# RWKV-7 layer: the second four key blocks ordered behind the norm of the first four, and r's weights split three and four pieces ahead

## The chip, the cores and the metric

The kernel runs on one core of one Trainium2 chip. The metric is the device time of one execution in microseconds (us), as the median of several runs. The core's engines each work through a queue of their own, in order: PE (TensorE, matmuls and transposes), DVE (VectorE), ACT (ScalarE), POOL (GpSimd) and SP (SyncE, which issues most of the loads). An instruction waits on semaphores for those on other engines whose results it needs.

## The reference

The model has two mixing layers, each followed by a gated conv-MLP, on 512 tokens of 1024 features: first an RG-LRU layer, then an RWKV-7 layer. The change lies in the RWKV-7 layer, of which this is the part that matters:

```python
rkv = jnp.einsum('sbtd,sde->sbte', xs_rkv, w_rkv)
r, k, v = rkv[0], rkv[1], rkv[2]
w = -jax.nn.softplus(-(w0 + jnp.tanh(xw @ w1) @ w2).astype(f32)) - 0.5
decay = jnp.exp(-jnp.exp(w))
a = jax.nn.sigmoid((a0 + (xa @ a1) @ a2).astype(f32))
kk = (kf * k_k).reshape(bsz, seq, RWKV_H, RWKV_N)
kk = kk / jnp.maximum(jnp.linalg.norm(kk, axis=-1, keepdims=True), 1e-12)
kf = kf * (1.0 + (a - 1.0) * k_a)
y = _rwkv7_scan(rh, hs(decay), kh, vh, -kk, kk * ah)
# one step of the scan, for each of 16 heads of 64:
#   sa = S a_t;  S = S * w_t + sa b_t + v_t k_t;  y = S r_t
```

`kk` is normalised within each head, which needs the sum of squares of 64 features, and then a reciprocal.

## The kernel before

**Stages.** The stages run one after the other: the RG-LRU layer, its conv-MLP, the RWKV-7 layer (here from about 540 to 800 us), the second conv-MLP. A big product is in float32 accuracy from three matmuls: each operand is split in a high part and the rest, and `mm3` (L81) multiplies high by high, high by low and low by high. A weight comes in pieces of 512 KB that are numbered in the order of use. Each is loaded (`raw`, by SP), its high part is cast on ACT (`wh`, L123) and its low part made on DVE (`wl`, L127). `next_weights(ahead=2)` hands out piece i after it has put loads up to piece i + 3 and splits up to piece i + 2 in the queues (with an `ahead` of 4 or more, loads up to i + `ahead` + 2). All raw pieces, splits and many other tiles share one pool of 24 buffers (`b4`), so a load is issued when a buffer of the pool comes free.

**The RWKV-7 layer here.** The projections run in the order k (two products of four blocks of 128 features each), r (two products), v. Pieces 105 to 112 are k's, 113 to 120 are r's, and those from 121 on v's. The mixed inputs of a projection (`mt`, then its split `mix`) are made beside the product before it.

**What prepares the keys.** `prepare(g)` in `rwkv_krv` (L1193) works on four of the eight blocks: g = 0 on the first four, g = 1 on the second. For each block b it makes exp of the running log decay and of its negative (`pinv` L1241 and `ppad` L1244, ACT), the square of the scaled keys (`sq` L1242, ACT), the factor of the second key (`fac` L1243, ACT), then `kp` (L1252, DVE), the other key's product (L1253, DVE), a copy of `ppad` (L1255, on ACT for g = 0, on DVE for g = 1) and two more products (L1257 and L1258, DVE), and PC (L1259, ACT). The squares are summed by a matmul (`ssq`, L1251). Behind the four blocks follows the norm, one dependent chain: ACT copies ssq to `tmp` (L1262), PE transposes it (`sst`, L1266), DVE takes the maximum and two reciprocals (L1268, L1270), PE transposes back (`rec`, L1274), ACT and DVE split it (L1276, L1277), PE spreads it over the heads (`knb`, L1283), and DVE multiplies it in (L1284). Two buffers each of ppad and pinv and one each of fac and kp serve all eight blocks.

**The solve.** `solve(H, ...)` makes the matrices of the heads: matmuls `aab` (L1353), copies of them on ACT (D0, DA and O, L1358 to L1362), a transpose on DVE (`A`, L1366), then a chain of pairs of DVE steps (L1374 and L1376) that invert a triangle row by row in X, then two transposes (LT, L1379, and XN, L1381). PE takes XN with the matmul `m1p` (L1400), and POOL makes the next solve's X out of LT. DVE also does for each chunk the products `W` (L1497) and `tu` (L1579), which PE takes in `tr` (L1504) and `pe` (L1534); `pd` (L1572) and `s` (L1490) lie between.

**Order.** The program is written as tasks that yield; `project` steps the tasks on two lanes while it issues its matmuls. `prepare(0)` and `prepare(1)` stand on lane 0 and `solve(0)` on lane 1:

```python
        self.push(prepare(0))
        ...
        self.push(prepare(1))
        self.push(self.solve(0, AR, BK, LTs), 1)
        self.project(mr, lambda o, ps: ev_r(o, ps), rate=0.4, rate1=1.2)
        self.project(mr, lambda o, ps: ev_r(4 + o, ps), after=trail(2, mv, (4, 2, 2, 2)), rate=1.3, rate1=0.9)
```

The order of the code is not yet that of the queues: a scheduler (Tile) orders each engine's instructions by when its model sees them ready, and the kernel can add a dependency without a semaphore ("NOSYNC") that only fixes an order.

Of the kernel before, what the change touches and what calls it, by code (L numbers as in the profile page):

```python
# [9 lines left out]
AF = mybir.ActivationFunctionType  # L10
ALU = mybir.AluOpType
# [3 lines left out]
NOSYNC = mybir.DependencyInfo(mybir.DependencyClass.NoSync, mybir.DependencyReason.DATA)  # L15
# [7 lines left out]
C = 64  # L23
# [3 lines left out]
DECAY_C = 0.6065306597126334  # L27
# [44 lines left out]
class Kernel:  # L72
# [991 lines left out]
    @staticmethod  # L1064
    def bytok(t):
        return t.rearrange("p (c q t) -> p c q t", q=2, t=C)
# [127 lines left out]
    def rwkv_krv(self, pool, mk, mr, AR, BK, PC, selk, LTs):  # L1194

        nc = self.nc

        def t(tag, bufs):
            return pool.tile([P, T], F32, tag=tag, name=tag, bufs=bufs)


        sel = pool.tile([P, 4, 40], F32, name="sel")
        n8 = pool.tile([P, 4, 40], F32, name="n8")
        for m in (sel, selk, n8):
            nc.gpsimd.memset(m, 0.0)
        for e in range(2):
            hb = slice(e * 64, e * 64 + 64)
            for b in range(4):
                for part in (0, 32):
                    c = part + 2 * b + e  # L1210
                    nc.gpsimd.memset(sel[hb, b, c : c + 1], 1.0)
            for b in range(KB):
                nc.gpsimd.tensor_copy(selk[hb, b, e : e + 1], self.vec("rwkv_r_k", b)[hb])
        backs = []

        def selection():
            psb = self.bank("back")
            for j in range(4):
                nc.tensor.transpose(psb[0:40, j * P : (j + 1) * P], sel[:, j, :], self.ident)
            backs.append(self.b4(F32R, (4 * P,), "back")[0:40])  # L1220
            nc.scalar.copy(backs[0], psb[0:40, :])

        ppads = [pool.tile([P, NC, C + 1], F32, name=f"ppad{i}") for i in range(2)]
        for pp in ppads:
            nc.vector.memset(pp[:, :, 0:1], 1.0)
        bytok = self.bytok

        def prepare(g):


            ssq = self.bank("ssq")
            sqs = []
            for j in range(4):
                b = g * 4 + j
                pad = ppads[b % 2]
                pp = pad.rearrange("p (c q) t -> p c q t", q=2)
                Lc, rr, a, ko = self.inner(AR, b), self.outer(AR, b), self.inner(BK, b), self.outer(BK, b)
                if j % 2 == 0:
                    two = self.b4(F32, (2, T), "sq")
                sq, pinv, fac, kp = two[:, j % 2], t("pinv", 2), t("fac", 1), t("kp", 1)  # L1240
                nc.scalar.activation(bytok(pinv), Lc, AF.Exp, scale=DECAY_C)  # L1241
                nc.scalar.activation(bytok(sq), ko, AF.Square, scale=self.vec("rwkv_k_k", b))  # L1242
                nc.scalar.activation(bytok(fac), a, AF.Identity, bias=self.oka[:, b : b + 1], scale=self.vec("rwkv_k_a", b))  # L1243
                nc.scalar.activation(pp[:, :, :, 1:], Lc, AF.Exp, scale=-DECAY_C)  # L1244
                yield 1
                if g == 0 and j == 2:
                    selection()

                sqs.append(sq)
                for i in (3, 0, 1, 2) if j == 3 else ():  # L1250
                    (self.tc.keep_in_program_order if i < 3 else lambda ins: ins)(nc.tensor.matmul(ssq[32 * i : 32 * i + 32, :], sel[:, 0, 0:32], sqs[i], start=True, stop=True, tile_position=(0, 32 * i)))  # L1251
                nc.vector.tensor_tensor(bytok(kp), ko, bytok(pinv), ALU.mult)  # L1252
                nc.vector.scalar_tensor_tensor(a, a, self.vec("rwkv_k_k", b), bytok(kp), ALU.mult, ALU.mult)  # L1253
                yield 1
                (nc.vector.tensor_copy if g else nc.scalar.copy)(rr, pp[:, :, :, 1:])  # L1255
                self.done.add(("r", b))
                nc.vector.tensor_tensor(Lc, ko, pp[:, :, :, 0:C], ALU.mult)  # L1257
                nc.vector.tensor_tensor(ko, bytok(kp), bytok(fac), ALU.mult)  # L1258
                nc.scalar.copy(PC[:, b, :], pad[:, :, C])  # L1259
                yield 1  # L1260
            ss = t("tmp", 1)
            nc.scalar.copy(ss, ssq)  # L1262
            yield 1
            pt = self.bank("sst")
            for c in range(4):
                nc.tensor.transpose(pt[:, c * P : (c + 1) * P], ss[:, c * P : (c + 1) * P], self.ident)  # L1266
            pv = pt.rearrange("p (c j w) -> p c j w", c=4, w=32)[:, :, :, 0:2]
            nc.vector.tensor_scalar(n8[:, :, 0:8].rearrange("p c (j e) -> p c j e", e=2), pv, 1e-24, None, ALU.max)  # L1268
            for part in (32, 0):
                nc.vector.reciprocal(n8[:, :, part : part + 8], n8[:, :, 0:8])  # L1270
            yield 1
            pr = self.bank("rec")
            for c in range(4):
                nc.tensor.transpose(pr[0:40, c * P : (c + 1) * P], n8[:, c, :], self.ident)  # L1274
            rec = self.b4(F32R, (T,), "rec")[0:40]
            nc.scalar.copy(rec, pr[0:40])  # L1276
            nc.vector.tensor_tensor(rec[32:40], pr[32:40], rec[32:40].bitcast(F32), ALU.subtract)  # L1277
            yield 1
            for j in range(4):
                b = g * 4 + j  # L1280
                Lc = self.inner(AR, b)
                pb = self.bank("knb")
                nc.tensor.matmul(pb, backs[0][:, j * P : (j + 1) * P], rec, start=True, stop=True)  # L1283
                nc.vector.scalar_tensor_tensor(Lc, Lc, self.nkk[:, b : b + 1], bytok(pb), ALU.mult, ALU.mult)  # L1284
                if j == 3:
                    self.done.add(("prepare", g))
                if j % 2:
                    yield 1

        def ev_r(b, ps):  # L1290
            self.need(("r", b))
            rr = self.outer(AR, b)
            nc.vector.tensor_tensor(rr, bytok(ps), rr, ALU.mult)

        def trail(i, out, counts):
            gen = self.mixes(i, out)
            return lambda c: [next(gen, None) for _ in range(counts[c])]

        self.push(prepare(0))
        mv = []  # L1300
        self.project(mk, lambda o, ps: nc.scalar.copy(self.outer(BK, 4 + o), bytok(ps)), after=trail(0, mr, (0, 0, 2, 2)), rate=1.2, ahead=3)
        self.push(prepare(1))
        self.push(self.solve(0, AR, BK, LTs), 1)
        self.project(mr, lambda o, ps: ev_r(o, ps), rate=0.4, rate1=1.2)
        self.project(mr, lambda o, ps: ev_r(4 + o, ps), after=trail(2, mv, (4, 2, 2, 2)), rate=1.3, rate1=0.9)
        self.tasks[0].extend(self.tasks[1])
        self.tasks[1].clear()
        return mv
# [568 lines left out]
```

## Time and profile before

| What | Value |
|---|---|
| median of 3 runs | 1262.08 us (1262.06 to 1263.38) |
| the profiled execution's own time | 1261.37 us |
| its span in the trace | 1259.7 us |
| granted TensorE clock, mean of that execution | 0.998 of full speed |
| ACT busy | 677.4 us, 54% of the span |

The page gives busy times over the whole span. A row of the timeline reads: start, duration, engine, line, operation, output<-input with shapes, and in brackets how long the engine was idle before the row and what ended that idle time. A row of the windows reads: the stretch, its length, then PE, PEld (weight loads), DVE, ACT and POOL busy with the number of instructions, the granted clock, the share of DMA and GB/s.

### The profile page before, as it was taken

The page shows a single profiled execution, that of the slowest core. Times are in us where ns is not written, and L with a number is a line of the kernel's source. Part 1 is how long each engine was busy: PE and PEld are TensorE (multiplying, and loading weights), DVE is VectorE, ACT ScalarE, POOL GpSimd, SP SyncE. Part 2 cuts the span into 40 slices and gives each one's busy share as a digit, 9 for nine tenths or more (in the row PEclk, how much of TensorE's full clock was granted, in tenths as well). Part 3 has the DMA queues.
Part 4 walks back from the last instruction along what each step waited for, and adds up shares of the span by engine and source line. Part 5 has one row for each costly group of instructions (what it writes and reads, how often), then busy time and mean ns, then how long its engine had stood idle before and what let it go on. Part 6 is the DMA issues. An engine that isn't in the chain of part 4 may idle for free.

```text
span 1259.7 us, 23711 instructions
## 1 busy us (share of the span) xinstructions
PE 1233.5 (98%) x9795; PEld 1076.8 (85%) x9795; DVE 974.0 (77%) x1465; ACT 677.4 (54%) x1074; POOL 132.4 (11%) x210
## 2 busy tenths in 40 slices
PE   9999999999999999999999999999999999999997
PEld 7777888999999998878678888778889999999986
DVE  7988687777777776989999966778766777777764
ACT  6697466444444444668745355545754444444442
POOL 0000000000000000020012054410000010000000
PEclk9999999999999999999999999999999999999999
DMA  7312233666676664502212112122236666666631
GB/s 259 101 67 84 100 103 84 183 178 174 169 174 172 179 175 140 174 25 78 84 47 81 51 48 86 62 85 88 96 84 184 170 173 177 171 174 174 177 126 67
DMA packets 47661, 158.31 MB, mean 126 GB/s; under 512 B 6112, under 2 KB 8416, under 8 KB 47424
## 3 DMA queue, kind: packets, MB, share of 16 engines
q1 hardware_dynamic: 38768, 126.37, 30.1%
q0 software_dynamic: 7920, 28.84, 13.4%
q8 instruction: 77, 1.26, 0.4%
q10 hardware_dynamic: 864, 1.57, 0.4%
q14 instruction: 32, 0.26, 0.1%
HBM read 152.24 MB, written 4.52 MB: 124 GB/s over the span
## 4 chain that ended last, share of the span: by engine, by line
PE 44%; DVE 4%; ACT 3%; issue 2%; POOL 1%; POOLq 0%; ACTq 0%; DVEq 0%
PE accA L81 8%; PE acc L81 6%; PE accF L81 4%; PE acc L893 3%; PE acc L894 3%; PE acc L892 3%; PE accU L81 3%; PE accG L81 3%; PE accD L81 2%; DVE X L1376 1%; PE s L1490 1%; DVE DA L1374 1%; PE pd L1572 1%; PE acc L1322 1%; PE pe L1534 1%
## 5 line engine op out<-in xcount | busy, mean ns | idle before, releaser
L127 DVE TENSOR_TENSOR wl<-raw,wh 128x1024 fp32r<-128x1024 f32 (+1 forms) x129 | 155.3, 1211 | 26.3 <-ACT wh L123 24.5
L775 DVE TENSOR_TENSOR lo<-raw,hi 128x1024 fp32r<-128x1024 f32 x126 | 150.9, 1219 | 14.0 <-PE accU L81 10.0
L81 PE MATMUL accA<-xt,hi 128*128 128x256 f32 x864 | 153.4, 280 | 0.0
L123 ACT CAST wh<-raw 128x1024 fp32r<-128x1024 f32 (+1 forms) x128 | 131.3, 1044 | 14.9 <-PE acc L81 5.1
L775 ACT CAST hi<-raw 128x1024 fp32r<-128x1024 f32 x126 | 128.5, 1048 | 12.2 <-PE acc L893 5.8
L81 PEld LDWEIGHTS accA<-xt,hi 128*128 128x128 f32 x864 | 131.4, 188 | 0.0
L81 PE MATMUL accA<-xt,lo 128*128 128x256 f32 x432 | 120.8, 280 | 0.0
L81 PE MATMUL acc<-hid,wh 128*128 128x512 f32 x384 | 118.1, 390 | 0.0
L802 ACT COPY s<-accA 128x512 f32<-128x512 f32 x54 | 31.7, 587 | 159.1 <-PE accA L81 159.0
L719 ACT ACTIVATE cv<-gpad,pv 128x512 f32<-128x512 f32 x48 | 37.2, 811 | 120.4 <-DVE gpad L822 113.4
L81 PEld LDWEIGHTS accA<-xt,lo 128*128 128x128 f32 x432 | 82.4, 191 | 0.0
L81 PEld LDWEIGHTS acc<-hid,wh 128*128 128x128 f32 x384 | 70.3, 188 | 13.0
L81 PE MATMUL acc<-xs,wh 128*128 128x512 f32 x248 | 77.8, 395 | 1.1 <-ACT wh L123 1.1
L893 PE MATMUL acc<-wh,hid 128*128 128x512 f32 (+1 forms) x200 | 76.2, 381 | 0.0
L894 PE MATMUL acc<-wl,hid 128*128 128x512 f32 (+1 forms) x200 | 76.2, 381 | 0.0
L892 PE MATMUL acc<-wh,hid 128*128 128x512 f32 (+1 forms) x200 | 76.2, 381 | 0.0
L81 PE MATMUL acc<-hid,wl 128*128 128x512 f32 x192 | 74.5, 390 | 0.0
L206 POOL DMA_DIRECT2D raw<-in_weights_dram x36 | 31.8, 882 | 366.7 <-DMA raw<-in_weights_dram 121.3
L721 DVE SCALAR_TENSOR_TENSOR cv<-gpad,pv,cv 128x512 f32<-128x512 f32 x96 | 67.1, 745 | 2.6 <-ACT cv L719 2.5
L81 PE MATMUL acc<-mix,wh 128*128 128x512 f32 x192 | 59.7, 393 | 1.6 <-ACT wh L123 1.6
L81 PE MATMUL accU<-xs,wh 128*128 128x512 f32 x192 | 59.8, 393 | 0.0
L81 PE MATMUL accG<-xs,wh 128*128 128x512 f32 x192 | 59.8, 392 | 0.0
(380 smaller groups left out, 3182.6 us busy)
## 6 DMA issues: line engine op xcount, KB each, us to landing
raw<-in_weights_dram SPq DMA_DIRECT2D x217, 512.0 KB, 3.8
raw<-in_weights_dram POOLq DMA_DIRECT2D x54, 512.0 KB, 6.6
xd<-x SPq DMA_DIRECT2D x8, 256.0 KB, 2.2
AR<-xd SPq DMA_DIRECT2D x1, 2048.0 KB, 8.9
x<-in_xT_dram SPq DMA_DIRECT2D x3, 512.0 KB, 6.8
out_dram<-xtok ACTq DMA_DIRECT2D x4, 256.0 KB, 2.1
out_dram<-xtok SPq DMA_DIRECT2D x4, 256.0 KB, 2.0
raw<-in_weights_dram SPq DMA_DIRECT2D x2, 256.0 KB, 4.8
```

Source lines behind the costliest of these rows:

```text
L81: mm = lambda *a, **kw: self.nc.tensor.matmul(ps, *a, skip_group_check=more, **kw)
L123: put = (self.nc.vector.tensor_copy if dve else self.nc.scalar.copy)(hi, src)
L127: rest = self.nc.vector.tensor_tensor(lo, src, hi.bitcast(F32), ALU.subtract)
L206: self.nc.gpsimd.dma_start(raw, more, accum_op=ALU.add)
L719: nc.scalar.activation(cv, pair.gp[:, e, 0:T], AF.Identity, bias=self.vec(f"ffn_conv_b{l}", fb), scale=cw(0))
L721: nc.vector.scalar_tensor_tensor(cv, pair.gp[:, e, j : j + T], cw(j), cv, ALU.mult, ALU.add)
L775: pair.at[p] = nc.scalar.copy(hi, f[p]), tt(lo, f[p], hi.bitcast(F32), ALU.subtract)
L802: copied = nc.scalar.copy(s[p], bank["A"])
L892: nc.tensor.matmul(ps, hh[:, s], wh[:, k, m], start=kk == 0, stop=False)
L893: nc.tensor.matmul(ps, hl[:, s], wh[:, k, m], start=False, stop=False)
L894: nc.tensor.matmul(ps, hh[:, s], wl[:, k, m], start=False, stop=kk == blocks - 1)
L1322: nc.tensor.matmul(ps, hh[:, s], wh[:, k, :], start=kk + b % 2 == 0, stop=False)
```

## The change

The instructions stay the same in kind and number. `prepare` puts an order on part of its work with `held`: what is made in `prepare(1)` gets a dependency without semaphore on the last instruction named in `tail`, which `prepare(0)` sets to the ssq copy (ACT) and to its second reciprocal (DVE). Held on ACT are pinv, sq, fac and ppad, on DVE kp, the copy of ppad and the two products of L1257 and L1258; the product of L1253 is not. The two products of r get `ahead=3` and `ahead=4`.

```diff
+        tail = {}
+
+        def held(key, ins):
+            if key in tail:
+                self.tc.add_manual_dep(ins.ins, tail[key].ins.name, NOSYNC, reason="order")
+            return ins
+
         def prepare(g):
-
+            act = lambda *a, **kw: held("act", nc.scalar.activation(*a, **kw))
+            dve = lambda ins: held("dve", ins)
...
-                nc.scalar.activation(bytok(pinv), Lc, AF.Exp, scale=DECAY_C)
-                nc.scalar.activation(bytok(sq), ko, AF.Square, scale=self.vec("rwkv_k_k", b))
+                act(bytok(pinv), Lc, AF.Exp, scale=DECAY_C)
+                act(bytok(sq), ko, AF.Square, scale=self.vec("rwkv_k_k", b))
...
-                nc.vector.tensor_tensor(bytok(kp), ko, bytok(pinv), ALU.mult)
+                dve(nc.vector.tensor_tensor(bytok(kp), ko, bytok(pinv), ALU.mult))
                 nc.vector.scalar_tensor_tensor(a, a, self.vec("rwkv_k_k", b), bytok(kp), ALU.mult, ALU.mult)
                 yield 1
-                (nc.vector.tensor_copy if g else nc.scalar.copy)(rr, pp[:, :, :, 1:])
+                if g:
+                    dve(nc.vector.tensor_copy(rr, pp[:, :, :, 1:]))
+                else:
+                    nc.scalar.copy(rr, pp[:, :, :, 1:])
...
-                nc.vector.tensor_tensor(Lc, ko, pp[:, :, :, 0:C], ALU.mult)
-                nc.vector.tensor_tensor(ko, bytok(kp), bytok(fac), ALU.mult)
+                dve(nc.vector.tensor_tensor(Lc, ko, pp[:, :, :, 0:C], ALU.mult))
+                dve(nc.vector.tensor_tensor(ko, bytok(kp), bytok(fac), ALU.mult))
...
-            nc.scalar.copy(ss, ssq)
+            copied = nc.scalar.copy(ss, ssq)
...
-                nc.vector.reciprocal(n8[:, :, part : part + 8], n8[:, :, 0:8])
+                last = nc.vector.reciprocal(n8[:, :, part : part + 8], n8[:, :, 0:8])
+            tail.update(act=copied, dve=last)
...
-        self.project(mr, lambda o, ps: ev_r(o, ps), rate=0.4, rate1=1.2)
-        self.project(mr, lambda o, ps: ev_r(4 + o, ps), after=trail(2, mv, (4, 2, 2, 2)), rate=1.3, rate1=0.9)
+        self.project(mr, lambda o, ps: ev_r(o, ps), rate=0.4, rate1=1.2, ahead=3)
+        self.project(mr, lambda o, ps: ev_r(4 + o, ps), after=trail(2, mv, (4, 2, 2, 2)), rate=1.3, rate1=0.9, ahead=4)
```

The queues change as follows at three places (line numbers of the changed kernel are 8 to 12 higher, and its four held activations carry the line of the helper `act`, L1236). First ACT around the norm of the first four blocks, from the PC copy at about 600.4 us to the copy of ssq. The tiles AR1 and BK1 are those of the second four blocks. Before:

```order
L1259 COPY PC_5234<-ppad1_5570 128x8
L1244 ACTIVATE ppad0_5569<-AR1_5242 128x8x64
L1243 ACTIVATE fac_5884<-BK1_5244,oka_371,pv_80 128x512
L1259 COPY PC_5234<-ppad0_5569 128x8
L1241 ACTIVATE pinv_6020<-AR1_5242 128x512
L1244 ACTIVATE ppad1_5570<-AR1_5242 128x8x64
L123 CAST wh113_5688<-raw113_5686 128x1024
L1301 COPY BK1_5244<-acc0_5573 128x4x2x64
L1262 COPY tmp_5734<-ssq_5589 128x512
```

And now:

```order
L1270 COPY PC_5234<-ppad1_5570 128x8
L123 CAST wh113_5688<-raw113_5686 128x1024
L1313 COPY BK1_5244<-acc0_5573 128x4x2x64
L1273 COPY tmp_5734<-ssq_5589 128x512
L1236 ACTIVATE pinv_5887<-AR1_5242 128x512
L1236 ACTIVATE fac_5888<-BK1_5244,oka_371,pv_80 128x512
L1236 ACTIVATE ppad0_5569<-AR1_5242 128x8x64
L1236 ACTIVATE pinv_6024<-AR1_5242 128x512
L123 CAST wh114_5694<-raw114_5692 128x1024
```

The two ppad, the fac, the pinv and the PC of the second four blocks stood ahead of the copy and now stand behind it; the pinv of the block before (not in the rows of before, two instructions further up) moved likewise.

Second, ACT at the norm of the second four blocks (about 650 us; equal neighbours drawn together). Before:

```order
L1242 ACTIVATE sq<-BK_5244,pv 128x512 x2
L123 CAST mix<-mt 128x512 x2
L1243 ACTIVATE fac<-BK_5244,oka,pv 128x512
L123 CAST mix<-mt 128x512 x2
L123 CAST wh_6183<-raw_6094 128x1024
L1262 COPY tmp<-ssq 128x512
```

And now:

```order
L1236 ACTIVATE sq<-BK_5244,pv 128x512 x2
L123 CAST mix<-mt 128x512 x2
L1236 ACTIVATE fac<-BK_5244,oka,pv 128x512
L123 CAST mix<-mt 128x512
L1273 COPY tmp<-ssq 128x512
```

Before and now a fac stands ahead of the copy. A fac waits for the product L1258 of the block before it, which reads the buffer that fac writes. Now DVE has the low halves of pieces 119 and 120 ahead of that L1258, which is L1269 in these rows (D0, A and X are the first solve's chain):

```order
L1386 TENSOR_TENSOR D0_5838<-A_5990,X_5992 128x231
L127 TENSOR_TENSOR wl119_6107<-raw119_6098,wh119_6106 128x1024
L1388 TENSOR_TENSOR X_5992<-X_5992,D0_5838 128x21x11
L127 TENSOR_TENSOR wl120_6111<-raw120_6100,wh120_6110 128x1024
L1386 TENSOR_TENSOR D0_5838<-A_5990,X_5992 128x240
L1269 TENSOR_TENSOR BK1_5244<-kp_6123,fac_6122 128x4x2x64
```

Before, the low half of 119 was the first of these two on DVE, and it stood behind the L1258 of the last block. Third, DVE at the end of the first solve (about 683 us). Before:

```order
L1374 TENSOR_TENSOR D0_5834<-A_5986,X_5988 128x31
L1376 TENSOR_TENSOR X_5988<-X_5988,D0_5834 128x31
L1379 STREAM_TRANSPOSE LT0_6591<-X_5988 128x32x32
L1381 STREAM_TRANSPOSE XN_6593<-X_5988 128x32x32
L1366 STREAM_TRANSPOSE DA_6438<-DA_6438 128x1024
L127 TENSOR_TENSOR wl124_6627<-raw124_6481,wh124_6626 128x1024
```

And now:

```order
L1388 TENSOR_TENSOR X_5992<-X_5992,D0_5838 128x3x29
L1378 STREAM_TRANSPOSE DA_6446<-DA_6446 128x1024
L1386 TENSOR_TENSOR D0_5838<-A_5990,X_5992 128x60
L1388 TENSOR_TENSOR X_5992<-X_5992,D0_5838 128x2x30
L1386 TENSOR_TENSOR D0_5838<-A_5990,X_5992 128x31
L1388 TENSOR_TENSOR X_5992<-X_5992,D0_5838 128x31
L1391 STREAM_TRANSPOSE LT0_6593<-X_5992 128x32x32
L1393 STREAM_TRANSPOSE XN_6595<-X_5992 128x32x32
```

The transpose of DA stood behind XN and now stands ahead of it, between two pairs of the chain.

More of the change, by code (lines that the diff above doesn't have):

```diff
@@ L1240, in prepare @@
                 sq, pinv, fac, kp = two[:, j % 2], t("pinv", 2), t("fac", 1), t("kp", 1)
-                nc.scalar.activation(bytok(pinv), Lc, AF.Exp, scale=DECAY_C)
-                nc.scalar.activation(bytok(sq), ko, AF.Square, scale=self.vec("rwkv_k_k", b))
-                nc.scalar.activation(bytok(fac), a, AF.Identity, bias=self.oka[:, b : b + 1], scale=self.vec("rwkv_k_a", b))
-                nc.scalar.activation(pp[:, :, :, 1:], Lc, AF.Exp, scale=-DECAY_C)
+                act(bytok(pinv), Lc, AF.Exp, scale=DECAY_C)
+                act(bytok(sq), ko, AF.Square, scale=self.vec("rwkv_k_k", b))
+                act(bytok(fac), a, AF.Identity, bias=self.oka[:, b : b + 1], scale=self.vec("rwkv_k_a", b))
+                act(pp[:, :, :, 1:], Lc, AF.Exp, scale=-DECAY_C)
                 yield 1
```

## The prediction

> **What bounds the kernel now.** I read the page first, for the engine that sets the end, then the table of windows around the changed code, then PE's timeline for its gaps, and last the rows of the engine that ended each gap.
>
> ```profile
> span 1259.7 us, 23711 instructions
> PE 1233.5 (98%) x9795; PEld 1076.8 (85%) x9795; DVE 974.0 (77%) x1465; ACT 677.4 (54%) x1074; POOL 132.4 (11%) x210
> 603.94:687.01 83.07, 76.87 (x637) 61.11 (x636) 80.45 (x157) 45.01 (x91) 9.16 (x20) 1.00 0.20 67
> 640.00:686.00 46.00, 45.92 (x392) 38.20 (x391) 45.43 (x99) 18.92 (x40) 5.98 (x17) 1.00 0.22 76
> 692.00:723.00 31.00, 29.38 (x555) 26.35 (x553) 29.02 (x74) 11.15 (x22) 3.81 (x8) 1.00 0.15 45
> ```
>
> PE is busy 98% of the span and the edit takes no matmul away, so only PE's gaps can be won. In the changed stretch (603.94 to 687.01) DVE is busy 80.45 of 83.07 us: it is nearly as full as PE, and the 77% of the page hides this. PE's gaps there and just behind are these:
>
> ```profile
> 604.92 0.66 PE L1266 MATMUL sst<-ident,tmp 128*128 128x128 f32 x4 [0.88 <-ACT tmp L1262]
> 610.13 0.60 PE L1274 MATMUL rec<-ident,n 128*40 128x128 f32 x4 [1.58 <-DVE n L1270]
> 613.86 1.21 PE L1283 MATMUL knb<-rec,back 40*128 40x512 f32 x4 [0.62 <-DVE rec L1277]
> 633.06 1.19 PE L81 MATMUL acc<-mix,wh 128*128 128x512 f32 x4 [1.59 <-ACT wh L123]
> 634.70 0.50 PE L81 MATMUL acc<-mix,wl 128*128 128x512 f32 x1 [0.45 <-DVE wl L127]
> 687.16 1.20 PE L1400 MATMUL m1p<-XN,O 32*32 32x32 f32 x64 [1.24 <-DVE XN L1381]
> 711.37 0.68 PE L1534 MATMUL pe<-tu,W 128*64 128x64 f32 x14 [1.16 <-DVE tu L1579]
> 725.74 0.66 PE L1504 MATMUL tr<-ident,BK 128*128 128x128 f32 x4 [1.47 <-DVE W L1497]
> ```
>
> The first five are 5.12 us. Between 640 and 686 PE does not wait at all. The last three belong to the triangular solves, which DVE carries.
>
> **First norm.** The work of the second four blocks leaves the queues ahead of the norm's copy and reciprocals.
>
> ```profile
> 598.87 0.62 ACT L1241 ACTIVATE pinv<-AR 128x512 f32<-128x512 f32 x1
> 600.48 0.63 ACT L1244 ACTIVATE ppad<-AR 128x512 f32<-128x512 f32 x1
> 602.35 0.62 ACT L1244 ACTIVATE ppad<-AR 128x512 f32<-128x512 f32 x1
> 604.28 0.58 ACT L1262 COPY tmp<-ssq 128x512 f32<-128x512 f32 x1
> 605.09 0.68 DVE L1252 TENSOR_TENSOR kp<-BK,pinv 128x512 f32<-128x512 f32 x1
> 606.29 0.74 DVE L1253 SCALAR_TENSOR_TENSOR BK<-BK,pv,kp 128x512 f32<-128x512 f32 x1
> 607.54 0.69 DVE L1257 TENSOR_TENSOR AR<-BK,ppad 128x512 f32<-128x512 f32 x1
> 608.50 1.23 DVE L127 TENSOR_TENSOR wl<-raw,wh 128x1024 fp32r<-128x1024 f32 x1
> 609.64 0.35 DVE L1270 RECIPROCAL n<-n 128x32 f32<-128x32 f32 x1
> 613.12 0.68 DVE L1277 TENSOR_TENSOR rec<-rec 8x512 fp32r<-8x512 f32 x1
> ```
>
> On ACT one pinv goes (598.87; such an operation takes 0.52 of the queue, its duration less the overlap with the next), and five instructions from the ppad at 600.48 through the one at 602.35 (602.35 + 0.52 - 600.48 = 2.39): together 2.9 us, so tmp starts at about 601.4 instead of 604.28, and PE's 0.88 goes, about 1.0 with a matmul that moves. On DVE five operations from 605.09 through 607.54 go (607.54 + 0.6 - 605.09 = 3.05, of which the n max, which stays, is 0.1). With the weights' wh early too, the second reciprocal, at 609.64 before, ends at about 606.7 instead of 610.0; PE, at it by 610.13 - 1.58 = 608.55 before, comes at about 606.7 (1.0 from the first gap, and some four matmuls fewer ahead of it) and waits about 0.2. The low half of rec keeps its distance of 3.5 us from the reciprocal (609.64 to 613.12), so knb follows at 610.6 instead of 613.86: PE is 3.3 us ahead.
>
> **Up to 640.** PE also has the copies of aab earlier, and the weights' casts behind them.
>
> ```profile
> 631.96 2.00 ACT L123 CAST wh<-raw 128x1024 fp32r<-128x1024 f32 x2
> 631.58 1.97 DVE L1366 STREAM_TRANSPOSE A<-D 128x1024 f32<-128x1024 f32 x1 [1.39 <-ACT D L1361]
> 643.23 0.39 PE L81 MATMUL acc<-mix,wl 128*128 128x512 f32 x1
> 643.45 0.39 PE L81 MATMUL acc<-early,wh 128*128 128x512 f32 x1
> raw<-in_weights_dram SPq DMA_DIRECT2D x217, 512.0 KB, 3.8
> ```
>
> The copies of aab (L1358 to L1362) follow knb through PE and end at about 629.7 on ACT, where the cast at 631.96 followed them before. The wh of weight piece 116 (r's first product takes 113 to 116) now stands among them, at about 628.2; its low half on DVE ends at 629.4. PE meets that piece at 629.45 where it met it at 634.70, with two matmuls fewer done (0.22 each, from 643.23 to 643.45): a gain of 4.8 us, nearly all of the 5.12. r's second product starts at about 638.6 instead of 643.45. The splits that come earlier need their loads earlier: SP issues each when its buffer comes free, which I place at 3 to 6 us ahead of the split; a load takes 3.8, so none is late by this estimate, and one that is costs PE at most those 3.8 once, out of a lead of 4.8.
>
> **Second norm.** It gives part back.
>
> ```profile
> 652.84 0.60 PE L1266 MATMUL sst<-ident,tmp 128*128 128x128 f32 x4
> ```
>
> ACT's fac of the last block now stands ahead of this tmp and waits for DVE's L1258 of the block before (it reuses that buffer), which stands behind two more low halves of r's weights (608.50 to 609.64, 1.14 each). I get the end of L1258 at 649.3, then fac, a cast and tmp in 1.9 us: 651.2. PE, ahead now, arrives at 652.84 - 3.2 = 649.6 and waits about 1.7 where it had no wait. Of 4.8 us some 3.2 remain. Behind tmp stands only DVE's n max, which has 3 us of other work ahead of it, so DVE does not wait here in this reading.
>
> **XN, the place that decides.** Before, DVE went from the transpose of A (ends 633.5) to XN without a wait:
>
> ```profile
> 645.27 0.35 DVE L1376 TENSOR_TENSOR X<-X,D 128x192 f32<-128x192 f32 x1
> 645.54 0.68 DVE L127 TENSOR_TENSOR mix<-mt,mix 128x512 fp32r<-128x512 f32 x1
> 684.98 2.03 DVE L1381 STREAM_TRANSPOSE XN<-X 128x1024 f32<-128x1024 f32 x1
> 686.89 1.92 DVE L1366 STREAM_TRANSPOSE DA<-DA 128x1024 f32<-128x1024 f32 x1
> 697.71 0.36 DVE L1376 TENSOR_TENSOR X<-X,DA 128x192 f32<-128x192 f32 x1
> 698.10 0.37 DVE L1374 TENSOR_TENSOR DA<-DA,X 128x207 f32<-128x207 f32 x1
> ```
>
> After, A ends at 631.6, 1.9 earlier. But what was held now lies between A and XN as well: two L1253 (606.29: 0.74, some 0.66 of the queue), one L1258, one L1257 and one L1252 (0.6 each), 3.1 us; the transpose of DA, which stood behind XN, stands ahead of it, 1.9; one low half less, -1.15; and eight more pairs of the chain stand side by side: a step holds the queue for 0.39 where the next step needs it (697.71 to 698.10) and for 0.27 where other work follows (645.27 to 645.54), 8 x 0.11 = 0.9. Sum 4.75, less 1.9: XN ends near 690.0 instead of 687.01. By the order of PE, 14 more matmuls of 256 columns stand ahead of m1p (half of 0.22 each and a little more, 1.7 us in all). PE arrives there at 684.4 (687.16 - 1.24 - 3.2 + 1.7) and waits 5.7 us where it waited 1.24. There PE is 3.0 - 1.7 = 1.3 us **later** than before: the gain is all back. The change does not make DVE's work less; it moves DVE's idle time to before A.
>
> **From m1p to 730.** The second solve's X starts with what POOL makes of LT:
>
> ```profile
> 691.78 0.21 DVE L1374 TENSOR_TENSOR DA<-DA,X 128x31 f32<-128x31 f32 x1 [1.87 <-POOL X L1370]
> 725.01 1.26 DVE L1497 TENSOR_TENSOR W<-s,masks 128x512 f32<-128x512 f32 x2
> 728.43 0.86 DVE L1579 TENSOR_TENSOR tu<-pd,decay 64x256 f32<-64x256 f32 x2 [1.02 <-PE pd L1572]
> ```
>
> LT ends about 2.8 later, so X's first step is at 694.6 (691.78). The W pair (1.2) and one low half (1.14) now stand ahead of the second LT: 694.6 + 33.3 (691.78 to 725.0) + 2.3 + 0.8 for the tu pair = 731.0, less the up to 2.0 us that DVE was idle from 692 to 723 (29.02 of 31.00). PE's gaps of 1.16 and 1.47 go, since W is early, and the next pe comes at 729.7 to 731.1 against about 729.3 + 0.4, with 0.6 of later matmuls done: a net of -0.6 to +0.8, say 0. Behind it the order is as before, and PE is bound by itself.
>
> **A long gap and the clock.** PE's new gap before m1p is longer than any near it.
>
> ```profile
> 786.40 0.33 PE L1572 MATMUL pd<-tu 128*64 128x64 f32 x1 [1.34 <-issue]
> 787.00:788.00 1.00, 0.81 (x15) 0.65 (x13) 0.99 (x3) 0.37 (x1) 0.96 (x2) 0.50 0.00 0
> ```
>
> After the gap that ends at 786.40 the granted clock was 0.50 for a few us. After a gap of 5.7 us I count up to 1.2 us from s through W to the second LT, half of it in the sum: +0.6. [...]
>
> **The rivals.**
> A (forecast): gain 4.8 to 640, repaid by XN; 0 + 0.6 us, its own range -0.6 to +1.6.
> B, DVE keeps up: XN at 690 hangs on some 5 us of DVE idle that I place ahead of A, where ACT's copies of aab end at 629.7. With the 80.45 us of work, 2.6 of idle as before and 0.9 of pairs from 601.0 on (2.9 before 603.94), XN ends at 685.0. Each us before 690 is a us at m1p and in the second solve: 3 to 5 us faster, about 1258.3 to the median. For it: the work is the same, and the splits give DVE early work. Against it: DVE's order is fixed, and A waited for ACT already (1.39).
> [...]
> C, slower: DVE waits at the second norm for rec. From the reciprocal to rec's low half took 3.5 us at the first norm (609.64 to 613.12); after the change only about 1.7 us of other work lies between them on DVE at the second, so it would idle up to 1.8, and XN, the second LT and PE move with it; with the clock's other 0.6 it is +2.4 to +3.2, about 1265. It decides once rec takes more than 1.7 us there.
> That the order does not change is excluded by the rows of the change: the held instructions do stand behind the copy and the reciprocals.
>
> **How the numbers follow.** A 0.54, B 0.29, C 0.17. The profiled execution took 1261.37 us (span 1259.7), 0.71 below the median 1262.08 of the runs shown; 1261.37 + 0.6 is 1262.0 on its scale, so 1262.7 beside that median. A alone is 1261.5 to 1263.7. About 0.2%, 2.5 us, can be told from no change: under 1259.6 or over 1264.6. Faster is most of B (0.24), slower most of C (0.13) and a tail of A (0.02), same the rest, 0.61. The range takes in B's middle and C: 1258.2 to 1265.0.
>
> **What would show it.** Right: tmp near 601.4, knb near 610.6, r's second product near 638.6, XN's end near 690 and a gap of 5 to 6 us before m1p with a clock below 1.00 behind it. Wrong: XN's end before 687 (B), or DVE idle at rec near 660 (C). If PE's gap at 633 stays, the first step fails, and the 4.8 with it.

## The result, and the profile after

The changed kernel took 1266.20 us (median of 10 runs, 1265.96 to 1271.05), the kernel before 1262.08 us (10 runs, 1261.44 to 1264.31): **slower by 0.39%** (ratio 1.0039, interval 1.0026 to 1.0051). The median is outside the predicted range of 1258.2 to 1265.0. The medians lie 4.1 us (0.33%) apart; the ratio takes in all ten runs. The longer of these runs had the lower mean clock: 1265.96 to 1266.25 us at 0.993 to 0.995, 1268.26 at 0.992, 1270.95 and 1271.05 at 0.989. The profiled execution took 1266.25 us, with a span of 1264.6 against 1259.7.

PE's timeline of the changed kernel has these waits where the prediction looked:

```profile
628.42 0.73 PE L81 MATMUL acc<-mix,wh 128*128 128x512 f32 x2 [0.43 <-ACT wh L123]
629.68 0.50 PE L81 MATMUL acc<-mix,wl 128*128 128x512 f32 x1 [0.53 <-DVE wl L127]
638.90 0.62 PE L81 MATMUL acc<-early,wh 128*128 128x512 f32 x2
651.00 0.66 PE L1277 MATMUL sst<-ident,tmp 128*128 128x128 f32 x4 [0.73 <-ACT tmp L1273]
686.12 0.39 PE L1334 MATMUL acc<-wh,mix 128*128 128x256 f32 x1 [0.59 <-ACT wh L123]
690.79 3.62 PE L1412 MATMUL m1p<-XN,O 32*32 32x32 f32 x128 [4.17 <-DVE XN L1393]
734.95 0.69 PE L1546 MATMUL pe<-tu,W 128*64 128x64 f32 x16 [2.47 <-DVE tu L1591]
```

The three waits of the first norm are gone, and r's second product starts at 638.90 instead of 643.45, 4.55 us ahead. At m1p PE stands still for 4.17 us, and it does so again, for 2.47, at the third pe (the matmul group that takes tu and W), which comes at 734.95 where it came at 729.67:

```profile
729.67 0.69 PE L1534 MATMUL pe<-tu,W 128*64 128x64 f32 x16
```

From 4.5 us ahead PE has gone to 5.3 us behind. The rest of the kernel keeps that (span +4.9).

The windows of one microsecond of the same execution show what PE's clock did (columns as in the prediction; the granted clock stands ahead of the last two numbers):

```profile
687.00:688.00 1.00, 0.00 (x0) 0.00 (x0) 0.97 (x2) 0.00 (x0) 0.00 (x0) 0.98 0.15 33
688.00:689.00 1.00, 0.00 (x0) 0.00 (x0) 1.00 (x2) 0.00 (x0) 0.00 (x0) 0.50 0.86 307
693.00:694.00 1.00, 1.00 (x46) 1.00 (x42) 0.00 (x0) 0.89 (x2) 0.94 (x2) 0.50 0.00 0
697.00:698.00 1.00, 1.00 (x14) 0.78 (x13) 1.00 (x1) 0.00 (x0) 0.00 (x0) 0.50 0.00 0
698.00:699.00 1.00, 1.00 (x52) 1.00 (x52) 0.90 (x5) 0.00 (x0) 0.00 (x0) 0.90 0.00 0
737.00:738.00 1.00, 1.00 (x20) 0.66 (x16) 0.33 (x1) 0.65 (x2) 0.91 (x2) 0.50 0.00 0
```

The clock is halved from 688.0 to 698.2, 10.2 us, although PE has work again from 690.8 on: for 7.4 us PE works at a granted clock of 0.50, and v's matmuls of 256 columns follow each other every 0.21 us up to 697.1 where they do every 0.12 us from 699.5 on. It halves once more behind the wait at 734.95, for 3.4 us (735.75 to 739.16). Before, it was 1.00 in both places.

DVE's timeline shows how the second solve got late (the last row is of the kernel before):

```profile
629.54 2.08 DVE L1378 STREAM_TRANSPOSE A<-D 128x1024 f32<-128x1024 f32 x1
684.15 2.04 DVE L1378 STREAM_TRANSPOSE DA<-DA 128x1024 f32<-128x1024 f32 x1 [0.69 <-ACT DA L1373]
688.80 1.93 DVE L1393 STREAM_TRANSPOSE XN<-X 128x1024 f32<-128x1024 f32 x1
695.59 0.21 DVE L1386 TENSOR_TENSOR DA<-DA,X 128x31 f32<-128x31 f32 x1 [3.31 <-POOL X L1382]
709.60 1.29 DVE L1509 TENSOR_TENSOR W<-s,masks 128x512 f32<-128x512 f32 x2 [2.02 <-PE s L1502]
732.22 1.90 DVE L1391 STREAM_TRANSPOSE LT<-X 128x1024 f32<-128x1024 f32 x1
723.21 1.95 DVE L1379 STREAM_TRANSPOSE LT<-X 128x1024 f32<-128x1024 f32 x1
```

XN ends at 690.73, 3.7 us later than before (687.01), 1.97 of it by DA's transpose ahead of it (684.15 to 686.12) and 0.69 by the wait of that transpose. X of the second solve starts 3.8 us later than before. Then DVE waits 2.02 us for PE's s. PE makes s at 708.41 to 709.54, at full clock again (1.00 from 708.4 to 709.6), but comes to it late, with the work that the half clock held up ahead of it; that wait was not there before. The second LT starts at 732.22 instead of 723.21, 9.0 us later. Two windows, from X's first step to the start of that LT, before and now, show where the time between them went:

```profile
691.78:723.21 31.43, 29.81 (x558) 26.66 (x559) 29.41 (x75) 11.37 (x22) 4.00 (x8) 1.00 0.15 45
695.59:732.22 36.63, 35.91 (x659) 32.54 (x658) 32.09 (x79) 13.93 (x29) 6.20 (x12) 0.96 0.19 60
```

DVE works 2.7 us more in it (the W pair and a low half now stand ahead of LT) and is idle for 4.5 us instead of 2.0.

### The profile page after: what moved, and what is told of

Same layout as the page of the kernel before. It is cut to its first block, busy times and chain, and to the rows that moved or that the text cites. A ratio compares the mean times of both kernels' runs of the same rounds, so it can differ in the third digit from the quotient of the medians.

```text
span 1264.6 us, 23710 instructions
## 1 busy us (share of the span) xinstructions
PE 1237.5 (98%) x9795; PEld 1080.2 (85%) x9795; DVE 975.6 (77%) x1465; ACT 677.2 (54%) x1074; POOL 132.5 (10%) x210
## 4 chain that ended last, share of the span: by engine, by line
PE 43%; DVE 6%; ACT 3%; issue 1%; POOL 0%; POOLq 0%; ACTq 0%; DVEq 0%
PE accA L81 8%; PE acc L81 5%; PE accF L81 4%; PE acc L893 3%; PE acc L894 3%; PE acc L892 3%; PE accU L81 3%; PE accG L81 3%; PE accD L81 2%; PE acc L1334 1%; PE s L1502 1%; PE acc L1336 1%; PE acc L1335 1%; DVE X L1388 1%; DVE wl L127 1%
```

## Experiments

**Theory 1 (clock).** Late XN opens a long gap ahead of m1p; the gap halves PE's clock; at half clock PE hands s to DVE late, so the second LT and the third pe are late too. **Theory 2 (order).** DVE's order in the solves (DA ahead of XN, W and a low half ahead of the second LT) costs all of it, and the clock is a by-product. Each run was timed beside the kernel before, in five rounds (the last one shown here in three); a ratio is to the kernel before in the same rounds, whose median lay between 1262.08 and 1262.50.

**The hold alone.**

```diff
-        self.project(mr, ..., rate1=1.2, ahead=3)
-        self.project(mr, ..., rate1=0.9, ahead=4)
+        self.project(mr, ..., rate1=1.2)
+        self.project(mr, ..., rate1=0.9)
```

> The hold without the earlier splits (both products of r split two pieces ahead, as before). Theory 1 (clock): the loss is paid by the half clock behind the late XN; here the transpose of DA stands behind XN again, so XN comes about 2 us earlier, the gap before m1p is under 3 us, the clock stays 1.00 there, and of the first norm's 3 us some stay: 1259 to 1262. Theory 2 (order of the second solve): no statement on the norm; 1262 to 1264.

Measured: 1260.88 us, ratio 0.9987 (0.9979 to 0.9996). **The earlier splits alone.**

```diff
-            tail.update(act=copied, dve=last)
```

> The earlier splits without the hold. DVE's work between A and XN is here of the same kind and number as in the changed kernel, and the transpose of DA stands ahead of XN. Theory 1: XN is as late as or later than in the changed kernel, the gap before m1p is 4 to 6 us, the clock falls to 0.50 behind it, and the first norm's gaps are back: 1266 to 1269. If the hold were what costs, this would be 1262 or less.

Measured: 1270.36 us, ratio 1.0069 (1.0055 to 1.0083). The first fence is of the hold alone, the second of the splits alone:

```profile
688.54 1.20 PE L1412 MATMUL m1p<-XN,O 32*32 32x32 f32 x64 [0.76 <-DVE XN L1393]
690.00:700.00 10.00, 10.00 (x245) 9.48 (x244) 7.64 (x21) 5.42 (x9) 4.69 (x5) 1.00 0.31 100
630.00:640.00 10.00, 9.02 (x31) 7.03 (x32) 8.62 (x17) 4.89 (x7) 0.00 (x0) 0.83 0.00 0
```

```profile
693.80 3.63 PE L1411 MATMUL m1p<-XN,O 32*32 32x32 f32 x128 [4.14 <-DVE XN L1392]
690.00:700.00 10.00, 6.20 (x140) 6.14 (x141) 6.45 (x10) 3.35 (x5) 6.88 (x8) 0.61 0.18 54
```

The hold is a gain by itself, 0.13%; the splits are the loss. With the hold alone XN's gap is 0.76 and the clock from 690 to 700 was 1.00; with the splits alone there is the same gap of 4.1 as in the changed kernel, with some 13.8 us of half clock behind it (by the means of 0.61 from 690 to 700 and 0.70 from 700 to 710). The hold alone has one half clock too, of 3.4 us from 632.5 on (the mean of 0.83 in its second window), behind a wait of 1.51 us for r's weights.

**DA's transpose behind XN.**

```diff
-        nc.vector.transpose(A, D0.rearrange("p u t -> p t u"))
+        turned = nc.vector.transpose(A, D0.rearrange("p u t -> p t u"))
+        if H:
...
+            self.tc.add_manual_dep(turned.ins, self.xn_made.ins.name, NOSYNC, reason="order")
...
-        nc.vector.transpose(xn.rearrange("p u s -> p s u"), X.rearrange("p t s -> p s t"))
+        self.xn_made = nc.vector.transpose(xn.rearrange("p u s -> p s u"), X.rearrange("p t s -> p s t"))
```

> The change with one more order: DA's transpose behind XN's on DVE. Both theories: XN ends about 2 us earlier (688.7), the gap before m1p shrinks by as much. Theory 1: if the clock then stays at 1.00, 4 us more come back and the time is about 1260.5; if it still halves, about 1264.3. Theory 2: 1264.3 with either clock.

Measured: 1263.98 us, ratio 1.0026 (1.0015 to 1.0037), 2.2 us under the changed kernel. In its profiled execution, which at 1268.09 us was one of the slowest of the eleven:

```profile
688.57 3.27 PE L1415 MATMUL m1p<-XN,O 32*32 32x32 f32 x128 [1.67 <-DVE XN L1396]
690.00:700.00 10.00, 10.00 (x160) 9.43 (x154) 7.95 (x20) 4.50 (x7) 3.88 (x5) 0.50 0.01 2
711.48 1.29 DVE L1512 TENSOR_TENSOR W<-s,masks 128x512 f32<-128x512 f32 x2 [6.16 <-PE s L1505]
```

The gap fell to 1.67 and the clock was halved nevertheless, for 17.1 us (689.1 to 706.2), and DVE waited 6.16 us for s. The median agrees with the branch "if it still halves, about 1264.3", but theory 2 gave 1264.3 as well: the time of this run does not tell the two apart.

**PE kept busy in the gap.** 40 transposes of the identity are added ahead of m1p, in the bank that m1p overwrites.

```diff
-                    nc.tensor.matmul(ps, hh[:, s], wh[:, k, :], start=kk + b % 2 == 0, stop=False)
+                    self.token_mm = nc.tensor.matmul(ps, hh[:, s], wh[:, k, :], start=kk + b % 2 == 0, stop=False)
...
             pvs = [bank("m1p") for _ in range(2)]
+            for i in range(40 if H == 0 and g == 0 else 0):
+                fed = nc.tensor.transpose(pvs[0].rearrange("p u s -> p (u s)")[:, 0:P], self.ident, self.ident)
+                self.tc.add_manual_dep(fed.ins, self.token_mm.ins.name, NOSYNC, reason="order")
```

> The change with 40 transposes of the identity (128 columns, some 4.8 us) put on PE ahead of m1p of the first solve, into the bank that m1p overwrites: PE does not stand still in the gap, everything else is the same. Theory 1: the granted clock stays 1.00 from 686 to 700, s and W of the second solve come earlier, and the time falls by 3 to 4 us, to about 1262.5. Theory 2: the clock may stay, the time does not fall: 1266 or more.

Measured: 1263.83 us, ratio 1.0014 (1.0005 to 1.0022). Its rows of PE, windows and DVE:

```profile
684.36 4.53 PE L1411 MATMUL m1p<-ident 128*128 128x128 f32 x40
691.31 1.20 PE L1415 MATMUL m1p<-XN,O 32*32 32x32 f32 x64 [2.42 <-DVE XN L1393]
690.00:700.00 10.00, 8.69 (x256) 8.17 (x258) 6.42 (x13) 4.52 (x7) 7.26 (x8) 1.00 0.16 48
696.07 0.21 DVE L1386 TENSOR_TENSOR DA<-DA,X 128x31 f32<-128x31 f32 x1 [3.31 <-POOL X L1382]
730.16 2.02 DVE L1391 STREAM_TRANSPOSE LT<-X 128x1024 f32<-128x1024 f32 x1
696.07:730.16 34.09, 32.37 (x617) 29.05 (x616) 32.11 (x78) 12.52 (x26) 6.13 (x12) 1.00 0.20 58
```

XN and X are no earlier than in the changed kernel (696.07 against 695.59), but the clock stays 1.00, DVE's wait for s does not appear, and the second LT starts 34.1 us behind X instead of 36.6. So added matmuls that do nothing **save 2.4 us** by the medians, and theory 2 fails as a full account. The run changes one thing besides the clock: 14 of v's matmuls fall behind m1p (108 stand ahead of it, as before the change, and 122 in the changed kernel). They give PE 1.7 us more to do between m1p and s, and s still starts 0.95 us earlier (707.46 against 708.41); this order delays s, so the earlier s is the clock's doing. What the order is worth behind s was not tried apart. By the medians the clock's share is under the 3 to 4 us of theory 1, by the ratios (1.0039 and 1.0014) it is 3.2; with intervals of 0.1% to each side the size is rough.

**Both.** DA's transpose behind XN, and the 40 transposes.

> The change with DA's transpose behind XN and the 40 transposes of the identity on PE ahead of m1p. Theory 1: clock and order are two terms that add up: the clock's 2.4 us (the changed kernel less the one with the transposes) and DVE's 2 us of DA, so 1261.5 to 1262.5, with the clock at 1.00 up to 740. If the 1.3 us gaps leave the clock halved nevertheless: 1264.

Measured: 1262.28 us, ratio 0.9999 (0.9991 to 1.0008).

```profile
725.46 2.00 DVE L1393 STREAM_TRANSPOSE LT<-X 128x1024 f32<-128x1024 f32 x1
727.31 1.26 DVE L1514 TENSOR_TENSOR W<-s,masks 128x512 f32<-128x512 f32 x2
710.00:720.00 10.00, 8.16 (x135) 7.35 (x133) 9.72 (x21) 1.52 (x5) 0.80 (x2) 0.83 0.20 55
```

By the medians 2.4 us of clock and 1.5 us of DA's place are 3.9 of the 4.1 that the change lost; taken in the other order (DA's place first, 1263.98, then the transposes) they are 2.2 us of DA's place and 1.7 of clock. DA's place here includes what follows from it: W and the low half stand behind the second LT again. The clock was expected to stay at 1.00 up to 740 and did not: it was halved for 3.4 us from 715.1 on, behind a wait of 1.84 us.

**Which of the two splits.** With the hold, three pieces ahead in the first product only; then four in the second only; then three in both.

```diff
-        self.project(mr, ..., rate1=1.2, ahead=3)
-        self.project(mr, ..., rate1=0.9, ahead=4)
+        self.project(mr, ..., rate1=1.2, ahead=3)  # left out in the second run
+        self.project(mr, ..., rate1=0.9, ahead=3)  # left out in the first run, 4 in the second
```

> The hold, with r's first product split three pieces ahead and the second two. DA's transpose stands behind XN. Theory 1 (a long gap before m1p throttles PE): the gap of 1.5 at the first product's wh that is left in the kernel with the hold alone shrinks to about 0.5, XN is no later than 688.5, the clock stays 1.00: 1259 to 1260.5, 1 us under the kernel with the hold alone. If the first product's earlier splits are what makes DVE late: over 1262.

> The hold, with r's first product split two pieces ahead and the second four. The first product's gap of 1.5 stays, that of 1.9 at the second product's wh goes. If the four pieces ahead in the second product are what brings the loss (DVE's W and low half ahead of the second LT, and a long gap before m1p): 1263 to 1266. If both settings together are needed for it: 1260 to 1261.5.

> The hold, with three pieces ahead in both products of r. DA's transpose stands behind XN by the schedule itself. Both gaps at r's weights shrink. Theory 1: the gap before m1p is under 3 us and the clock mostly stays 1.00: 1259 to 1262. If DVE's order alone costs: 1263 to 1265.

Measured: 1261.04 (0.9991, 0.9983 to 1.0000), 1262.02 (1.0004, 0.9994 to 1.0014) and 1261.85 us (0.9999, 0.9990 to 1.0008). No one of them loses the 0.39%: that takes three and four together, which is where DA's transpose comes ahead of XN. None gains over the hold alone (1260.88) either. In the first, PE's wait of 1.5 at the first product's wh shrank to 0.43 as expected, and the wait at the second product's wh grew (1.90 with the hold alone):

```profile
628.64 0.73 PE L81 MATMUL acc<-mix,wh 128*128 128x512 f32 x2 [0.43 <-ACT wh L123]
662.51 2.61 PE L81 MATMUL acc<-mix,wh 128*128 128x512 f32 x8 [2.71 <-ACT wh L123]
688.36 1.20 PE L1412 MATMUL m1p<-XN,O 32*32 32x32 f32 x64 [0.94 <-DVE XN L1393]
```

The m1p of the kernel with the hold alone comes at 688.54, of this one at 688.36: the lead is used up by then. The second's profiled execution shows the clock within one kernel. It took 1266.35 us at a mean clock of 0.992, where the median of its runs is 1262.02 (those from 1261.75 to 1262.08 had 0.996). A gap of 1.37 was followed by 10.2 us of half clock, and DVE then waited 3.41 us for s; the runs near the median left no trace to set beside it:

```profile
689.15 1.20 PE L1412 MATMUL m1p<-XN,O 32*32 32x32 f32 x64 [1.37 <-DVE XN L1393]
690.00:700.00 10.00, 10.00 (x175) 9.48 (x169) 8.00 (x19) 4.52 (x7) 4.37 (x6) 0.54 0.01 2
709.77 1.29 DVE L1509 TENSOR_TENSOR W<-s,masks 128x512 f32<-128x512 f32 x2 [3.41 <-PE s L1502]
```

**What sets XN.** The copies of ppad of the second four blocks go from DVE to ACT (in the changed kernel they lie ahead of A); in another kernel two products of L1269 go from DVE to POOL (they lie between A and XN).

```diff
-                    dve(nc.vector.tensor_copy(rr, pp[:, :, :, 1:]))
+                    held("act", nc.scalar.copy(rr, pp[:, :, :, 1:]))
```

```diff
-                dve(nc.vector.tensor_tensor(ko, bytok(kp), bytok(fac), ALU.mult))
+                (nc.gpsimd.tensor_tensor(ko, bytok(kp), bytok(fac), ALU.mult) if g and j > 1 else dve(nc.vector.tensor_tensor(ko, bytok(kp), bytok(fac), ALU.mult)))
```

> The change, with the copies of ppad of the second four blocks (4 x 0.42 us) on ACT instead of DVE. They lie ahead of A on DVE, where DVE waits anyway. If XN is set by where A ends plus the list of work behind it: XN does not move (within 0.5 us of 690.7) and the time stays at 1265.5 to 1266.5. If DVE's sum of work sets XN (the reasoning behind rival B): XN 1.6 us earlier, 1264 or, where the clock stays, 1262.

> The change, with the product of L1269 of the last two blocks on POOL, so that two operations (2 x 0.6 us) leave DVE between A and XN. If that list sets XN: XN ends 1.0 to 1.3 us earlier, the time falls by as much, and by 2 more where the clock then stays: 1263 to 1265. If something else does (a wait for POOL's slower product at fac or at the norm): no gain, 1266 or more.

Measured: 1266.54 us (1.0046, 1.0031 to 1.0060) and 1270.31 us (1.0066, 1.0054 to 1.0078). The row is of the first:

```profile
691.06 3.62 PE L1412 MATMUL m1p<-XN,O 32*32 32x32 f32 x128 [4.17 <-DVE XN L1393]
```

Taking 1.7 us off DVE ahead of A brought neither A nor m1p forward (A ends at 632.04 and m1p starts at 691.06, 0.4 and 0.3 us later than in the changed kernel): it is not DVE's sum of work that sets XN but A's place and the list behind it. The POOL kernel was to show the other half and did not, since POOL brought a cost of its own:

```profile
650.43 2.27 POOL L1269 TENSOR_TENSOR BK<-kp,fac 128x512 f32<-128x512 f32 x1 [8.63 <-DVE kp L1260]
651.45 1.80 DVE L1261 SCALAR_TENSOR_TENSOR BK<-BK,pv,kp 128x512 f32<-128x512 f32 x1
660.35 0.87 PE L1286 MATMUL rec<-ident,n 128*40 128x128 f32 x4 [3.11 <-DVE n L1281]
```

The product took 1.73 and 2.27 us on POOL (0.68 on DVE), and a DVE operation beside it 1.80 where its like took 0.74. XN ended 2.4 us later than in the changed kernel. How much of that is the longer operation and how much the order around it stays open.

**The hold with the copies on ACT, and two variants.** The hold alone with the copies of ppad on ACT; the hold alone with 12 transposes of the identity at the wait of 1.5 us; the first of these with three pieces ahead in r's first product.

```diff
...
+            if fed and len(cs) > 1:
+                ps = self.bank("fed")
+                for i in range(fed):
+                    self.nc.tensor.transpose(ps[:, 0:P], self.ident, self.ident)
...
+        self.project(mr, lambda o, ps: ev_r(o, ps), rate=0.4, rate1=1.2, fed=12)
```

> The hold alone, with the copies of ppad of the second four blocks on ACT. With the hold alone one of them lies between A and XN, so 0.4 us are saved there: 1260.0 to 1260.9. If ACT's copies delay A's inputs: 1261 to 1262.

> The hold alone, with 12 transposes of the identity on PE (1.4 us) ahead of the first product's third weight piece, where PE waits 1.5 us for wh. Theory 1: a part of the executions with the hold alone lose 1.5 to 2 us to a half clock behind that wait (its times lie in two groups, 1259.1 to 1260.1 and 1260.9 to 1262.8); with PE kept busy the median falls to 1259.5 or less. If the clock there costs nothing: 1260.9 as before, or more by the transposes that overrun the wait.

> The hold, the copies of ppad of the second four blocks on ACT, and r's first product split three pieces ahead. The wait of 1.9 us for wh in the first product that is left without the earlier splits goes to about 0.5. If PE's waits there are worth their length: 1258.5 to 1259.5. If, as with the hold alone, DVE hands it back later: 1259.8 to 1260.3, the same as without them.

Measured: 1259.86 (0.9979, 0.9970 to 0.9987), 1260.70 (0.9988, 0.9979 to 0.9997) and 1260.78 us (0.9987, 0.9978 to 0.9996). The first fence is of the first, the second of the one with the transposes:

```profile
687.49 1.20 PE L1412 MATMUL m1p<-XN,O 32*32 32x32 f32 x64 [1.35 <-DVE XN L1393]
630.00:640.00 10.00, 8.60 (x31) 6.95 (x32) 8.74 (x16) 6.12 (x10) 0.00 (x0) 0.83 0.01 2
```

```profile
630.00:640.00 10.00, 8.79 (x38) 6.72 (x37) 10.00 (x21) 6.08 (x9) 0.00 (x0) 1.00 0.01 2
```

The first is **the best version, 0.21% under the kernel before**; its m1p comes 1.05 us ahead of that of the hold alone, where 0.4 was expected. Its interval and that of the hold alone (0.9979 to 0.9996) overlap. The transposes did keep the clock at 1.00 where the hold alone and the best version have 3.4 us of half clock (0.83 as the mean of 630 to 640), but the median stayed within 0.2 us of the hold alone: PE's 0.2 for wh was followed by 1.0 for wl. So the half clock at that wait is not shown to cost anything. The third says again that earlier splits in the first product are handed back.

**Why the half clock lasts.** 16 transposes of XN, 128 by 128, ahead of m1p.

```diff
             pvs = [bank("m1p") for _ in range(2)]
+            for i in range(16 if H == 0 and g == 0 else 0):
+                nc.tensor.transpose(pvs[0].rearrange("p u s -> p (u s)")[:, 0:P], xn.rearrange("p u s -> p (u s)")[:, 0:P], self.ident)
```

> The change with 16 transposes of XN (128 by 128) on PE ahead of m1p of the first solve; they wait for XN, so the gap of 4.2 us stays. In the changed kernel the clock is 0.50 from 688.0 to 698.1 with PE busy from 690.8 on, first with m1p's 32 by 32 matmuls up to 694.3. If these do not release the clock: here wide work runs first (3.8 us at half clock), and the clock returns about 3.4 us earlier, near 694.8, so that the half clock lasts some 7 us. If only the gap counts: it lasts 10 us again. The time is 1266 to 1268 in either case, since the transposes themselves cost up to 3.8 us.

Measured: 1267.20 us (1.0040, 1.0024 to 1.0055), within the 1266 to 1268 of both readings; the length of the half clock fits neither. In its profiled execution, at 1270.22 us the longest of its four, the clock halved later and came back later than either had it:

```profile
691.09 3.67 PE L1411 MATMUL m1p<-ident,XN 128*128 128x128 f32 x16 [4.15 <-DVE XN L1393]
690.00:691.00 1.00, 0.00 (x0) 0.00 (x0) 1.00 (x2) 0.00 (x0) 0.94 (x2) 0.58 0.00 0
694.00:695.00 1.00, 1.00 (x16) 0.67 (x16) 0.00 (x0) 0.00 (x0) 0.93 (x2) 0.50 0.00 0
707.00:708.00 1.00, 1.00 (x32) 0.96 (x29) 0.90 (x4) 0.39 (x1) 0.00 (x0) 0.89 0.00 0
```

Half clock from 690.2 to 707.2, 17.1 us, with wide matmuls at its start. Its three other runs had a mean clock of 0.996 to 0.997, where those of the changed kernel had 0.989 to 0.995, so in them it was shorter; one trace can't say why. The lengths have a pattern: by the clock in the windows of the traces they were 3.4 us (from 632.5 in the kernel with the hold alone, from 735.75 in the changed kernel), 6.8 at m1p of the changed kernel with the copies on ACT (a mean of 0.66 from 690 to 700), 10.2 at m1p of the changed kernel, some 13.8 with the splits alone and 17.1 here and in the run with DA behind XN: about one to five times the shortest. Why it was three times that in one execution and five in another **stays open**. The small matmuls of m1p and of the steps behind it may be part of it; that was not shown.

## Why the prediction was wrong

- **First norm and 640: right.** tmp started at 601.28 (601.4 predicted), knb at 610.51 (610.6), r's second product at 638.90 (638.6). The gain of 4.8 us was 4.55, and the first waits were taken away as reasoned.
- **Second norm: right in kind, smaller.** tmp started at 650.36 and PE waited 0.73 for it, not 1.7. v's product started 3.5 us ahead of before (665.23 against 668.75), where 3.2 were left by the sum.
- **XN: right.** It ended at 690.73 (690.0 predicted, 687.01 before), with DA's transpose ahead of it. The waits ahead of m1p were 0.59 and 4.17 us; 5.7 were predicted in one. The kernel with the copies on ACT shows that the list behind A sets XN, as the sum had it, and not DVE's sum of work, on which rival B stood. B fails with it.
- **From m1p to 730: wrong by 4 us, and the first step that failed.** The third pe was put at 729.7 to 731.1 and came at 734.95. X's start was 1.0 late (695.59 for 694.6). From X's first step to the end of the second LT the sum had the 33.3 us of before and 2.3 for the W pair and the low half, less up to 2.0 us in which DVE had been idle; it became 38.5 (to 734.12). The added work came as counted (2.7 us more busy), but DVE's idle time grew from 2.0 to 4.5 us instead of going, 2.02 of it in the new wait for s. With PE kept busy it was 2.0 again (32.11 of 34.09 busy): even at full clock none of it paid for the W pair and the low half.
- **The clock: the second step that failed.** "After a gap of 5.7 us I count up to 1.2 us from s through W to the second LT, half of it in the sum: +0.6." The effect is named there, the size is wrong: the half clock lasted 10.2 us, where the one behind 786.40 in the kernel before lasted 3.4 (786.46 to 789.88), PE came late to s by it, and behind the 2.47 us gap that followed came another, of 3.4 us. Keeping PE busy in the gap gave back 2.4 us by the medians, four times the 0.6. No run shows the 1.2 us or the half of it: both were the author's estimate. The prediction let the length of the gap decide, which was not shown either: gaps of 1.37 and 1.67 us were followed by 10.2 and 17.1 us of half clock, one of 4.17 by 10.2, while the clock stayed at 1.00 behind the 1.59 at 633.06 in the kernel before and behind 1.90 at 664.46 in the one with the hold alone. In the changed kernel the clock fell at 688.0, when PE had stood still for 1.3 us (since 686.62), with 0.5 us of work and a wait of 0.59 ahead of that; PE was busy from 690.8 and had the full clock back only at 698.2, 7.4 us later.
- **DA's place** was in the sum for XN, but as a part of something that PE's lead would pay for. By the run with DA behind XN and PE kept busy it is worth 1.5 us at the end, with the W pair and the low half back behind the second LT. Clock and DA together are 3.9 of the 4.1 us.
- **C**, the slower rival, named the wrong place. The wait at the second norm's rec that it stood on did not come: DVE's low half of rec starts at 660.40, as soon as the operation ahead of it (659.63, 0.74 us) has ended. The chance of slower, 0.15, lay on a mechanism that did not happen.

## What to carry to other kernels

A gain on PE ahead of a stage that another engine carries is worth only what that stage can take: here 4.55 us of lead turned into a standstill at the next product of DVE. That standstill did not end with the wait of 4.17 us: the clock was at 0.50 for 7.4 us of the work behind it, and DVE then waited 2.02 us for s. Price one with the clock's recovery as seen in traces of the same kind of work (half clocks of 3.4 to 17.1 us here), and try to keep PE busy there if it can't be avoided: it paid 2.4 us at m1p, and no gain was shown at the wait of 1.5 us for r's weights. What an order moves on the second engine should be read up to that engine's next product, not only to the wait that it removes: with the order held and the splits left where they were, 0.13% was won, and 0.21% with the four copies of ppad moved to an engine that had time.

## What the runs showed of the hardware

- The half clock lasted 10.2 us (688.0 to 698.2) around a wait of 4.17 us, and 17.1 us in another kernel (690.2 to 707.2) around one of 4.15 us; PE's records are busy for all but the first 2.8 us of the one and the first 0.9 us of the other. The half clocks in the windows of the traces lasted 3.4, 6.8, 10.2, some 13.8 and 17.1 us, about one to five times the shortest. A gap of 1.37 us (four pieces ahead in r's second product only) was followed by half clock in one execution, which took 4.3 us more than the median of the same kernel; a wait of 2.42 us right behind 4.5 us of transposes was not (1.00 from 680 to 710).
- A product of 128x512 took 1.73 and 2.27 us on POOL and 0.68 on DVE, and a DVE operation that ran beside the longer one took 1.80 instead of 0.74.
